# The first group's upper output columns as one seven-product block, with the second group's lower columns inside it

## The chip, the cores and the metric

The kernel runs on one core of a Trainium2 chip. The metric is the device time of one execution in microseconds (us): the median of three runs before is 1700.65 (1699.88 to 1701.31). Engines are named as in the profile: PE (matrix multiply) and PEld (its weight loads), DVE (vector engine), ACT (scalar engine), POOL (GpSimd), SP (sync engine); each works through its own queue in order. SP's queue issues nearly all loads, POOL's the few that add to what lies in memory.

## The reference

One decoder layer for 256 tokens (S) of width 2048 (D), in float32: a SwiGLU FFN of half weight, a mixer, a second such FFN, with RMS norms between. What matters here is the mixer's end:

```
y = concatenate([rms_norm(y_lru, lru_out_norm[l]),
                 rms_norm(y_sc, sc_out_norm[l])], axis=-1)
x = x + y @ w_out[l]
x = x + FFN_RESIDUAL_SCALE * swiglu_ffn(rms_norm(x, ffn2_norm[l]), ...)
```

`y` has two groups of 1024 columns, each with a norm of its own, so the 2048 rows of `w_out` fall into two halves of the K dimension: rows 0 to 1023 belong to the first group, 1024 to 2047 to the second. Each half's product is scaled by its group's norm factor (one number per token) and added to the residual `x`.

## The kernel before

**Units.** A weight matrix is read in units of 512 rows by 512 columns (1 MiB), each by one DMA from SP (line 165) into one of three `raw` buffers. For full precision a unit is split in two: ACT casts it to the matmul's format (`hi`, two casts of half a unit), DVE subtracts (`lo = raw - hi`); there are two `hi`/`lo` buffer pairs (in the FFNs a third, used in every third turn). The activations are split likewise and lie transposed, in units of 512 rows: `yT_0`, `yT_1` for the first group and `yT_2`, `yT_3` for the second, each with both token tiles (t = 0, 1, of 128 tokens). `multiply` runs, for each token tile, 8 matmuls with `hi` and later 4 with `lo`, each 128x128 by 128x512: 24 matmuls for a unit and both tiles, 12 for one tile. Nearly all instructions carry line 43, that of a helper, so they are told apart by tiles.

**The output projection** is a loop over column blocks c (512 columns) and groups g in a fixed order: (0,0), (1,0), (0,1), (2,0), (1,1), (3,0), (2,1), (3,1). Each step (`product`) multiplies two units, `o{c}_{g}_{u}`, into two banks of PSUM (`ps_o`), and DVE adds both to the residual `xres` with the group's factor (`r_y0`, `r_y1`; from the tiny products `pst_0` and `pst_1` of the sums of squares `acc`). The first step of group 1 has its first load held until the mixer's last DMA transpose is issued. When a column block has both groups, it is complete, and the second FFN's input is prepared (`n2`): ACT copies the block's residual into `pair`, SP transposes it by DMA, ACT copies it back and scales it into `xT_n2`, DVE makes its `lo`, ACT sums squares (`junk`).

**Seven products.** In the FFNs, blocks of 2 x 2 units by 2 token tiles are done with seven instead of eight unit products (`seven`). With w11, w12 (upper row, first and second column block), w21, w22 (lower row) the weights multiplied are, in the order of the products p0, p4, p5, p6, p2, p3, p1: w11; w11+w12; that +w22; w12+w22; w22; that of p5 +w21; w21. DVE adds the sums into w11 in halves (`joined`), followed by ACT's cast and DVE's subtract of each half; w12+w22, and with `fourth` also the last +w21, are made by a DMA from POOL that adds in memory (`gather`). The activations' sums are made and split once (`seven_of`, `xs`). w11 and w12 lie in two buffers of their own (`kept`). The products go to three or four PSUM banks, a, c, d (and e), and `snap` copies a bank in between (s5, u2, u3) on ACT. With `beside`, four ordinary units of another product stand inside the block (first FFN's and second FFN's down projection, `down_pair`); then bank e isn't used.

**Order.** The program is written in one order, and a scheduler with costs of its own sets the order of the instructions within each engine's queue.

Of the kernel before, what the change touches and what calls it, by code (L numbers as in the profile page):

```python
# [49 lines left out]
def hybrid_block(ctx: ExitStack, tc: tile.TileContext, a: dict, out: bass.AP):  # L50
# [344 lines left out]
    def quad(tile):  # L395
        return tile.rearrange("p (j c) -> p j c", j=UK)

    def seven(w, rows, cols, sf, xs, name, keep, done, between=None, ready=None, whole=True, order=False, fourth=False, beside=None):
# [562 lines left out]
    with tc.tile_pool(name="mixer", bufs=1) as mp, tc.tile_pool(name="mixw", bufs=2) as mw:  # L961
# [15 lines left out]
        zx, gv, hs, vs, ds, ts, cc, ys, xcs = ({} for _ in range(9))  # L977
# [211 lines left out]
        n2 = Norm("n2", vec["ffn2_norm"])  # L1189
        w_out, turn = a["w_out"][0], held["turn"]  # L1190
        rs = []
        for c, g in [(0, 0), (1, 0), (0, 1), (2, 0), (1, 1), (3, 0), (2, 1), (3, 1)]:
            cs = slice(c * CW, (c + 1) * CW)
            if c == 0 and g == 1:
                flush()
            ps = product(w_out, c, (2 * g, 2 * g + 1), yT.__getitem__, f"o{c}_{g}", turn if (c, g) == (0, 1) else None)
# [9 lines left out]
            for t in range(NT):
                xr = xres[:, t, cs]
                dve.scalar_tensor_tensor(xr, ps[t], rs[g][:, t : t + 1], xr, op0=ALU.mult, op1=ALU.add)
            if g == 1:
                n2.later(c, lambda name: tmp("T", name, 4 * S)[:, :CW], False)  # L1210
# [91 lines left out]
```

## Time and profile before

| | |
|---|---|
| median of the runs | 1700.65 us |
| the profiled execution's own time | 1699.97 us |
| its span, first to last instruction | 1698.2 us |
| granted PE clock | 0.999 |
| busy: PE, DVE, ACT | 99%, 85%, 72% |
| output projection on PE | 919.87 to 1007.92 us of the span |
| input projection before it, second FFN behind it | up to 919.87, from 1007.92 |

Rows of a timeline give the start, the duration, the engine, the operation with output and input tiles, the count, and in brackets the idle time before and what ended it. Names lose their buffer numbers there: `ps_o`, `hi_o` and `raw_o` are the projection's, `hi_d_p` is the `hi` of one of seven products of a down projection.

### The profile page before, as it was taken

The numbers are of one execution on the slowest core, as the hardware profiler recorded it, in microseconds if no ns is written. First come the engines' busy times: TensorE is split into PE (matmuls) and PEld (weight loads), VectorE is DVE, ScalarE is ACT, GpSimd is POOL, SyncE is SP. The second block draws the span as 40 slices with busy tenths as digits, with TensorE's granted clock in tenths as the row PEclk, the third lists the DMA queues.
The fourth block names the chain that finished last, engine by engine and source line by source line (L and its number), as shares of the span: only waits on it lengthen the run. The fifth ranks groups of instructions, "written<-read, shape, count | busy, mean of one in ns | idle before, by whom it ended". The sixth has DMA issues, their size and how long they took to land.

```text
span 1698.2 us, 19673 instructions
## 1 busy us (share of the span) xinstructions
PE 1682.9 (99%) x7447; PEld 1391.6 (82%) x7447; DVE 1442.5 (85%) x1295; ACT 1228.1 (72%) x1534; POOL 47.9 (3%) x52
## 2 busy tenths in 40 slices
PE   8999999999999999999999999999999999999998
PEld 7888888888887888888888888888888888888886
DVE  7998988988988888768696669979889889899787
ACT  7867667758668677977877687776668578678764
POOL 1000000000000000000000000000000000000000
PEclk9999999999999999999999999999999999999999
DMA  8778679788788886875667587787778988888873
GB/s 304 239 249 228 221 245 244 234 256 241 232 279 230 253 262 160 249 215 195 206 203 223 196 248 220 240 249 223 247 234 236 271 234 239 249 246 247 247 226 124
DMA packets 271070, 396.67 MB, mean 234 GB/s; under 512 B 86404, under 2 KB 88832, under 8 KB 270848
## 3 DMA queue, kind: packets, MB, share of 16 engines
q1 hardware_dynamic: 253472, 360.49, 66.1%
q0 software_dynamic: 17216, 33.63, 11.5%
q8 instruction: 58, 0.95, 0.2%
q10 hardware_dynamic: 288, 1.31, 0.2%
q14 instruction: 36, 0.29, 0.1%
HBM read 373.37 MB, written 2.10 MB: 221 GB/s over the span
## 4 chain that ended last, share of the span: by engine, by line
PE 97%; DVE 2%; issue 0%; DMA 0%; ACT 0%; DVEq 0%; SPq 0%; ACTq 0%
PE ps_d L43 14%; PE ps_in L43 13%; PE ps_u_a L43 10%; PE ps_g_a L43 9%; PE ps_u_c L43 6%; PE ps_d_a L43 6%; PE ps_g_c L43 6%; PE ps_o L43 5%; PE ps_g_d L43 5%; PE ps_u_d L43 5%; PE ps_d_c L43 4%; PE ps_u_e L43 3%; PE ps_g_e L43 3%; PE ps_g L43 3%; PE ps_u L43 2%; PE ps_d_d L43 2%
## 5 line engine op out<-in xcount | busy, mean ns | idle before, releaser
L43 ACT CAST hi_u_p<-raw_u 128x1024 fp32r<-128x1024 f32 x140 | 143.0, 1046 | 79.6 <-PE ps_u_a L43 27.8
L43 DVE TENSOR_TENSOR lo_g_p<-raw_g,hi_g_p 128x2048 fp32r<-128x2048 f32 (+1 forms) x84 | 153.1, 1831 | 31.8 <-ACT hi_g_p L43 30.9
L43 DVE TENSOR_TENSOR lo_u_p<-raw_u,hi_u_p 128x2048 fp32r<-128x2048 f32 (+1 forms) x90 | 161.6, 1813 | 21.4 <-ACT hi_u_p L43 20.5
L43 PE MATMUL ps_d<-hi_d,h 128*128 128x512 f32 x704 | 167.2, 389 | 0.0
L43 ACT CAST hi_d_p<-raw_d 128x1024 fp32r<-128x1024 f32 x112 | 115.0, 1047 | 68.0 <-DVE raw_d L43 21.0
L43 ACT CAST hi_g_p<-raw_g 128x1024 fp32r<-128x1024 f32 x132 | 134.8, 1046 | 40.4 <-DVE raw_g L43 24.1
L43 PEld LDWEIGHTS ps_d<-hi_d,h 128*128 128x128 f32 x704 | 132.1, 188 | 27.4
L43 PE MATMUL ps_in<-hi_in,xT_nm 128*128 128x512 f32 x640 | 152.0, 390 | 0.0
L43 PEld LDWEIGHTS ps_in<-hi_in,xT_nm 128*128 128x128 f32 x640 | 119.5, 188 | 24.5
L43 DVE TENSOR_TENSOR lo_d_p<-raw_d,hi_d_p 128x2048 fp32r<-128x2048 f32 (+1 forms) x72 | 129.3, 1812 | 9.3 <-ACT hi_d_p L43 7.7
L43 DVE TENSOR_TENSOR lo_in<-raw_in,hi_in 128x2048 fp32r<-128x2048 f32 x40 | 91.2, 2286 | 45.3 <-ACT hi_in L43 44.9
L43 DVE TENSOR_TENSOR lo_d<-raw_d,hi_d 128x2048 fp32r<-128x2048 f32 x44 | 100.4, 2287 | 22.6 <-ACT hi_d L43 22.5
L43 ACT CAST hi_d<-raw_d 128x1024 fp32r<-128x1024 f32 x88 | 89.2, 1045 | 28.2 <-DMA raw_d<-in_ffn_w_down_dram 10.9
L43 ACT CAST hi_u_x<-raw_u 128x1024 fp32r<-128x1024 f32 x80 | 81.2, 1047 | 35.6 <-PE ps_u_c L43 26.2
L43 ACT CAST hi_in<-raw_in 128x1024 fp32r<-128x1024 f32 x80 | 80.7, 1047 | 27.5 <-PE ps_in L43 22.5
L43 ACT CAST hi_g_x<-raw_g 128x1024 fp32r<-128x1024 f32 x80 | 81.4, 1045 | 17.8 <-DMA raw_g<-in_ffn_w_gate_dram 8.6
L43 DVE TENSOR_TENSOR lo_g_x<-raw_g,hi_g_x 128x2048 fp32r<-128x2048 f32 x40 | 91.4, 2285 | 2.8 <-ACT hi_g_x L43 2.8
L43 DVE TENSOR_TENSOR lo_u_x<-raw_u,hi_u_x 128x2048 fp32r<-128x2048 f32 x40 | 91.4, 2285 | 1.4 <-ACT hi_u_x L43 1.3
L43 PE MATMUL ps_d<-lo_d,h 128*128 128x512 f32 x352 | 87.3, 389 | 0.0
L43 PE MATMUL ps_in<-lo_in,xT_nm 128*128 128x512 f32 x320 | 79.0, 389 | 0.0
L43 PEld LDWEIGHTS ps_d<-lo_d,h 128*128 128x128 f32 x352 | 66.1, 188 | 13.7
L43 DVE TENSOR_TENSOR raw_u<-raw_u,raw_u 128x1024 f32<-128x1024 f32 (+1 forms) x50 | 70.5, 1434 | 5.2 <-DMA raw_u<-in_ffn_w_up_dram 4.9
(405 smaller groups left out, 3683.3 us busy)
## 6 DMA issues: line engine op xcount, KB each, us to landing
raw_d<-in_ffn_w_down_dram SPq DMA_DIRECT2D x88, 1024.0 KB, 5.7
raw_u<-in_ffn_w_up_dram SPq DMA_DIRECT2D x87, 1024.0 KB, 5.2
raw_g<-in_ffn_w_gate_dram SPq DMA_DIRECT2D x86, 1024.0 KB, 5.5
raw_in<-in_w_in_dram SPq DMA_DIRECT2D x40, 1024.0 KB, 5.1
raw_o<-in_w_out_dram SPq DMA_DIRECT2D x16, 1024.0 KB, 5.5
raw_d<-in_ffn_w_down_dram POOLq DMA_DIRECT2D x12, 1024.0 KB, 8.3
raw_g<-in_ffn_w_gate_dram POOLq DMA_DIRECT2D x10, 1024.0 KB, 8.6
raw_u<-in_ffn_w_up_dram POOLq DMA_DIRECT2D x10, 1024.0 KB, 8.3
```

The costliest lines, as they stand in the source:

```text
L43: ins = getattr(self.engine, name)(*args, **kwargs)
```

## The change

Columns 1024 to 2047 (c = 2, 3) of the first group become one seven-product block named `ob`: rows (0, 1) of units, column blocks 2 and 3. The four units of the second group for c = 0 and 1 stand inside it (`Beside`). The order of the projection is now (0,0), (1,0), block with (0,1) and (1,1) inside, (2,1), (3,1). The block's sums of activations are made by `first_group_sums` from `yT_0` and `yT_1`, in the buffers of the mixer's v and d. Its third `hi`/`lo` pair and w11 (`kept_o`) take three of the ten `big` buffers, and w12 (`T_kept`) takes the mixer's T, whose two halves are now one tile; the crossings of `n2` move from T's buffers to the `tok` ones. w11's load is held until the last mixer transpose is issued, as the first load of group 1 was before; w12's is not held and waits for the last reader of T.

```diff
-    def product(w, c, us, y, name, after=None):
+    def product(w, c, us, y, name):
...
-            with tc.issue_after(after.ins) if after and i == 0 else ExitStack():
-                blk = unit(w[u * UK * P : (u + 1) * UK * P, cs], f"{name}_{u}")
+            blk = unit(w[u * UK * P : (u + 1) * UK * P, cs], f"{name}_{u}")
...
-        w11, first = ready or (get(r0, 0, True), None)
+        with tc.issue_after(first_load.ins) if first_load else ExitStack():
+            w11, first = ready or (get(r0, 0, True), None)
...
-                ts[half] = tmp("T", half, 4 * S)
+                both["T"] = both.get("T") or tmp("T", "both", 8 * S, bufs=1)
+                ts[half] = both["T"][:, half * 4 * S : (half + 1) * 4 * S]
...
-        for c, g in [(0, 0), (1, 0), (0, 1), (2, 0), (1, 1), (3, 0), (2, 1), (3, 1)]:
...
-            ps = product(w_out, c, (2 * g, 2 * g + 1), yT.__getitem__, f"o{c}_{g}", turn if (c, g) == (0, 1) else None)
...
+        def onto(c, g, t, *parts):
+            xr = xres[:, t, c * CW : (c + 1) * CW]
+            for p in parts:
+                dve.scalar_tensor_tensor(xr, p, rs[g][:, t : t + 1], xr, op0=ALU.mult, op1=ALU.add)
+
+        def column_done(c):
+            n2.later(c, lambda name: tmp("tok", name, CW, bufs=3), False)
+
+        def whole_product(c, g):
+            ps = product(w_out, c, (2 * g, 2 * g + 1), yT.__getitem__, f"o{c}_{g}")
+            if len(rs) == g:
+                group_factor(g)
+            for t in range(NT):
+                onto(c, g, t, ps[t])
+            if g == 1:
+                column_done(c)
+
+        def first_group_sums():
+            rows = [tmp(tag, "yv", 4 * S, bufs=1) for tag in "vd"]
+            for i in range(2):
+                y = f32(yT[i])
                 for t in range(NT):
+                    dve.tensor_tensor(
+                        quad(rows[t][:, i * CW : (i + 1) * CW]),
+                        y[:, :, t * P : (t + 1) * P], y[:, :, S + t * P : S + (t + 1) * P], op=ALU.add,
+                    )
+            so, two = {}, [big(f"xs_o_{i}") for i in range(2)]
+            rest = seven_of(
+                so, yT[0], yT[1],
...
+        def first_group_block(so, rest):
...
+                def load(i):
+                    c, u = i // 2, 2 + i % 2
+                    return load(w_out[u * UK * P : (u + 1) * UK * P, c * CW : (c + 1) * CW], f"o{c}_{u}")
...
+                def multiply(i, raw):
+                    c, u = i // 2, 2 + i % 2
+                    if u == 2:
+                        side[c] = [bank(f"ps_o{c}_{t}") for t in range(NT)]
+                    blk = parts_of(raw, f"o{c}_{u}")
+                    multiply([(side[c][t], stationary(yT[u], t), u == 2, u == 3) for t in range(NT)], blk, True)
+                    pump(1.5)
+                    if u == 3:
+                        if len(rs) == 1:
+                            group_factor(1)
+                        for t in range(NT):
+                            onto(c, 1, t, side[c][t])
+                        column_done(c)
...
+            def add(t, n, ps, tiles):
+                onto(2 + n, 0, t, *([] if ps is None else [ps]), *tiles)
...
+            extra.extend((
+                Given(hi=big("hi_o"), lo=big("lo_o")),
+                Given(kept=[f32(big("kept_o")), tmp("T", "kept", 8 * S, bufs=1).rearrange("p (j c) -> p j c", j=UK)]),
+            ))
+            seven(
+                w_out, (0, 1), (2 * CW, 3 * CW), so, [], "ob", keep, add, within, fourth=True, beside=Beside, first_load=turn,
+            )
+            extra.clear()
...
+        whole_product(0, 0)
+        sums_of_first = first_group_sums()
+        whole_product(1, 0)
+        flush()
+        first_group_block(*sums_of_first)
+        for c in (2, 3):
+            whole_product(c, 1)
```

What the scheduler made of it, at three places. On PE, from the last product before the block (columns 512 to 1023 of group 0) on, before:

```order
L43 MATMUL ps_o1_0_1_7061<-lo_o1_0_1_7101,yT_1_5359 128x512 x4
L43 MATMUL ps_o0_1_0_7131<-hi_o0_1_2_7135,yT_2_5360 128x512 x8
L43 MATMUL ps_o0_1_1_7132<-hi_o0_1_2_7135,yT_2_5360 128x512 x8
L43 MATMUL ps_o0_1_0_7131<-lo_o0_1_2_7136,yT_2_5360 128x512 x4
L43 MATMUL ps_o0_1_1_7132<-lo_o0_1_2_7136,yT_2_5360 128x512 x4
```

and now (`ps_ob_a`, `ps_ob_c` are the block's banks, `hi_ob_p0` the `hi` of product p0, `hi_o` the third buffer pair, here for the inner unit `o0_2`):

```order
L43 MATMUL ps_o1_0_1_7072<-lo_o1_0_1_7112,yT_1_5359 128x512 x4
L43 MATMUL ps_ob_a_7146<-hi_ob_p0_7163,yT_0_5358 128x512 x8
L43 MATMUL ps_ob_a_7146<-lo_ob_p0_7164,yT_0_5358 128x512 x4
L43 MATMUL ps_ob_c_7147<-hi_ob_p4_7181,xs_o_0_7065 128x512 x4
L43 MATMUL ps_o0_0_7213<-hi_o_7142,yT_2_5360 128x512 x3
L43 MATMUL ps_ob_c_7147<-hi_ob_p4_7181,xs_o_0_7065 128x512 x4
L43 MATMUL ps_ob_c_7147<-lo_ob_p4_7182,xs_o_0_7065 128x512 x2
```

p0 and p4 of the block stand where the first group-1 unit stood, and the inner unit `o0_2` is mixed into p4; behind them come `pst_1` and p5, mixed with the inner unit `o0_3`.

On DVE, from the first group's norm factor on, before:

```order
L43 SCALAR_TENSOR_TENSOR xres_76<-ps_o0_0_1_6953,r_y0_7051,xres_76 128x512
L43 TENSOR_TENSOR lo_o1_0_1_7101<-raw_o1_0_1_7098,hi_o1_0_1_7100 128x2048
L43 TENSOR_TENSOR lo_o0_1_2_7136<-raw_o0_1_2_7133,hi_o0_1_2_7135 128x2048
L43 SCALAR_TENSOR_TENSOR xres_76<-ps_o1_0_0_7060,r_y0_7051,xres_76 128x512
L43 SCALAR_TENSOR_TENSOR xres_76<-ps_o1_0_1_7061,r_y0_7051,xres_76 128x512
L43 TENSOR_TENSOR lo_o0_1_3_7167<-raw_o0_1_3_7164,hi_o0_1_3_7166 128x2048
```

and now (`kept_o` is w11, `T_kept` w12, `raw_ob_11` w22):

```order
L43 SCALAR_TENSOR_TENSOR xres_76<-ps_o0_0_1_6952,r_y0_7050,xres_76 128x512
L43 TENSOR_TENSOR lo_o1_0_1_7112<-raw_o1_0_1_7109,hi_o1_0_1_7111 128x2048
L43 TENSOR_TENSOR lo_ob_p0_7164<-kept_o_7144,hi_ob_p0_7163 128x2048
L43 TENSOR_TENSOR xs_o_0_7065<-v_yv_7059,xs_o_0_7065 128x4x128
L43 SCALAR_TENSOR_TENSOR xres_76<-ps_o1_0_0_7071,r_y0_7050,xres_76 128x512
L43 SCALAR_TENSOR_TENSOR xres_76<-ps_o1_0_1_7072,r_y0_7050,xres_76 128x512
L43 TENSOR_TENSOR kept_o_7144<-kept_o_7144,T_kept_7145 128x1024 x2
L43 TENSOR_TENSOR xs_o_1_7066<-d_yv_7060,xs_o_1_7066 128x4x128
L43 TENSOR_TENSOR lo_ob_p4_7182<-kept_o_7144,hi_ob_p4_7181 128x1024 x2
```

The two half-adds for p4 come behind both residual updates of columns 512 to 1023, and the second of them is what the first adding DMA on POOL (w22 into `T_kept`) waits for.

On ACT, behind the casts of the last unit before the block, before:

```order
L43 CAST hi_o0_1_2_7135<-raw_o0_1_2_7133 128x1024 x2
L43 CAST hi_o0_1_3_7166<-raw_o0_1_3_7164 128x1024 x2
L43 CAST hi_o2_0_0_7219<-raw_o2_0_0_7217 128x1024 x2
L43 CAST hi_o2_0_1_7256<-raw_o2_0_1_7254 128x1024 x2
L43 ACTIVATE s_y1_7201<-v_y1_7200 128x2
```

and now:

```order
L43 CAST hi_ob_p0_7163<-kept_o_7144 128x1024 x2
L43 CAST xs_o_1_7066<-v_yv_7059 128x4x128
L43 CAST hi_o_7142<-raw_o0_2_7151 128x1024 x2
L43 CAST hi_ob_p4_7181<-kept_o_7144 128x1024
L43 COPY ps_ob_d_7148<-ps_ob_a_7146 128x512
L43 CAST hi_ob_p4_7181<-kept_o_7144 128x1024
L43 ACTIVATE ctok_s5_ob_7202<-ps_ob_c_7147 128x512
L43 CAST hi_o_7142<-T_kept_7145 128x1024 x2
L43 CAST hi_ob_p5_7242<-kept_o_7144 128x1024 x2
L43 CAST hi_o0_3_7265<-raw_o0_3_7155 128x1024 x2
```

The casts of p6 (`hi_o` from `T_kept`, which the adding DMA writes and which the inner unit `o0_2` has to release) stand ahead of those of p5.

More of the change, by code (lines that the diff above doesn't have):

```diff
@@ L396, in quad, with seven @@
         return tile.rearrange("p (j c) -> p j c", j=UK)
-    def seven(w, rows, cols, sf, xs, name, keep, done, between=None, ready=None, whole=True, order=False, fourth=False, beside=None):
+    def seven(w, rows, cols, sf, xs, name, keep, done, between=None, ready=None, whole=True, order=False, fourth=False, beside=None, first_load=None):
         a, c, e, d = (bank(f"ps_{name}_{n}") if n != "e" or not beside else None for n in "aced")
@@ L976, in hybrid_block @@
         cw, scw = vec["lru_conv_w"], vec["sc_conv_w"]
-        zx, gv, hs, vs, ds, ts, cc, ys, xcs = ({} for _ in range(9))
+        zx, gv, hs, vs, ds, ts, cc, ys, xcs, both = ({} for _ in range(10))
         def tmp(tag, name, w=S, dt=F32, bufs=2):
@@ L1191, in hybrid_block, with group_factor @@
         rs = []
-        for c, g in [(0, 0), (1, 0), (0, 1), (2, 0), (1, 1), (3, 0), (2, 1), (3, 1)]:
-            cs = slice(c * CW, (c + 1) * CW)
-            if c == 0 and g == 1:
-                flush()
-            ps = product(w_out, c, (2 * g, 2 * g + 1), yT.__getitem__, f"o{c}_{g}", turn if (c, g) == (0, 1) else None)
-            if c == 0:
-                pst = bank(f"pst_{g}")
+        def group_factor(g):
+            pst = bank(f"pst_{g}")
+            for t in range(NT):
+                pe.matmul(pst[:, t : t + 1], acc[:, g, t * P : (t + 1) * P], ones[:, :1], start=True, stop=True)
+            tot = work.tile([P, NT], F32, tag="tot", name=f"tot_y{g}")
+            dve.tensor_copy(tot, pst[:, :NT])
+            rs.append(inv_sqrt(tot, D // 2, f"y{g}"))
@@ L1199, in hybrid_block @@
+        def first_group_sums():
+            rows = [tmp(tag, "yv", 4 * S, bufs=1) for tag in "vd"]
+            for i in range(2):
+                y = f32(yT[i])
                 for t in range(NT):
-                    pe.matmul(
-                        pst[:, t : t + 1], acc[:, g, t * P : (t + 1) * P], ones[:, :1], start=True, stop=True
-                    )
-                tot = work.tile([P, NT], F32, tag="tot", name=f"tot_y{g}")
-                dve.tensor_copy(tot, pst[:, :NT])
-                rs.append(inv_sqrt(tot, D // 2, f"y{g}"))
@@ L1206, in hybrid_block @@
[L1206 to L1210, printed above, removed]
+                    dve.tensor_tensor(
+                        quad(rows[t][:, i * CW : (i + 1) * CW]),
+                        y[:, :, t * P : (t + 1) * P], y[:, :, S + t * P : S + (t + 1) * P], op=ALU.add,
+                    )
@@ new lines, in first_group_sums, with __init__, tile @@
+            so, two = {}, [big(f"xs_o_{i}") for i in range(2)]
+            rest = seven_of(
+                so, yT[0], yT[1],
+                lambda t, i: quad(rows[t][:, i * CW : (i + 1) * CW]),
+                quad(tmp("tok", "yspare", CW, bufs=3)),
+                [(b[:, :, o : o + P], b[:, :, o + P : o + S]) for b in two for o in (0, S)],
+            )
+            return so, rest
+        class Given:
+            def __init__(self, **tiles):
+                self.tiles = tiles
+            def tile(self, shape, dt, tag, name, bufs):
+                return self.tiles[tag].pop(0) if tag == "kept" else self.tiles[tag]
@@ new lines, in first_group_block, with keep, within @@
+        def first_group_block(so, rest):
+            side = {}
+            class Beside:
+                @staticmethod
+                def load(i):
+                    c, u = i // 2, 2 + i % 2
+                    return load(w_out[u * UK * P : (u + 1) * UK * P, c * CW : (c + 1) * CW], f"o{c}_{u}")
+                @staticmethod
+                def multiply(i, raw):
[8 more added lines that the diff above has]
+                            group_factor(1)
+                        for t in range(NT):
+                            onto(c, 1, t, side[c][t])
+                        column_done(c)
+            def keep(name):
+                if name.startswith("u3"):
+                    return tmp("g", name, UK * S, bufs=1)[:, :CW]
+                return tmp("ctok", name, CW)
+            def add(t, n, ps, tiles):
+                onto(2 + n, 0, t, *([] if ps is None else [ps]), *tiles)
+            def within(i):
+                if i == 0:
+                    rest()
+            count = turn_of["split"]
+            turn_of["split"] = 0
+            extra.extend((
[6 more added lines that the diff above has]
+            extra.clear()
+            turn_of["split"] = count
```

## The prediction

> **What bounds the kernel now.** First the page: busy time by engine, and the shares of the chain of waits.
>
> ```profile
> PE 1682.9 (99%) x7447; PEld 1391.6 (82%) x7447; DVE 1442.5 (85%) x1295; ACT 1228.1 (72%) x1534; POOL 47.9 (3%) x52
> PE 97%; DVE 2%; issue 0%; DMA 0%; ACT 0%; DVEq 0%; SPq 0%; ACTq 0%
> ```
>
> TensorE is the chain for 97% of the span. Then the windows of the stretches that the change touches (start of the output projection, the rest of it, the first 42 us of the second FFN) and the PE timeline in it.
>
> ```profile
> core 0: us, PE busy (x) PEld busy (x) DVE busy (x) ACT busy (x) POOL busy (x), PEclk, DMA share, GB/s
> 919.80:942.00 22.20, 22.20 (x102) 18.40 (x101) 16.44 (x26) 17.74 (x25) 0.00 (x0) 1.00 0.63 194
> 942.00:1008.00 66.00, 66.00 (x295) 54.70 (x294) 41.77 (x52) 46.67 (x73) 0.00 (x0) 1.00 0.73 225
> 1008.00:1050.00 42.00, 42.00 (x189) 34.86 (x188) 40.31 (x57) 31.49 (x45) 0.00 (x0) 1.00 0.76 262
> ```
>
> ```profile
> 936.70 3.79 PE L43 MATMUL ps_o<-hi_o,yT 128*128 128x512 f32 x16
> 940.32 1.98 PE L43 MATMUL ps_o<-lo_o,yT 128*128 128x512 f32 x8
> 942.14 3.79 PE L43 MATMUL ps_o<-hi_o,yT 128*128 128x512 f32 x16
> 1007.92 3.79 PE L43 MATMUL ps_g<-hi_g,xT_n 128*128 128x512 f32 x16
> ```
>
> PE has no gap: 24 matmuls (one weight unit for both token tiles) take 942.14 - 936.70 = 5.44 us, 0.227 us each. DVE is about 65% busy and ACT 71% in the projection; behind it DVE is full, 40.31 of 42 us. So a matmul less is worth 0.227 us, and whatever makes PE wait costs its whole length.
>
> **The change part by part.** *Removed:* seven products instead of eight, 12 of the 384 projection matmuls: 12 x 0.227 = **-2.7 us**. That is the most the projection itself can give.
>
> *Start of the block.* p0's matmuls follow the last one of columns 512 to 1023, so PE is ready for p0 at 942.14 and for p4 at 944.86. Rows for what p4 needs:
>
> ```profile
> 928.04 0.37 SPq L165 DMA_DIRECT2D raw_o<-in_w_out_dram  x1
> DMA to landing us min/median/max: 7.6/7.6/7.6
> 935.45 1.41 DVE L43 SCALAR_TENSOR_TENSOR xres<-ps_o,r_y,xres 128x512 f32<-128x512 f32 x2
> 936.78 4.48 DVE L43 TENSOR_TENSOR lo_o<-raw_o,hi_o 128x2048 fp32r<-128x2048 f32 x2
> 317.22 0.68 DVE L43 TENSOR_TENSOR hs<-z,hs 128x512 fp32r<-128x512 f32 x1
> 320.62 2.35 DVE L43 TENSOR_TENSOR raw_d<-raw_d,raw_d 128x1024 f32<-128x1024 f32 x2
> ```
>
> The first row is the load after the last mixer transposes; the new load of kept_o is issued right behind one like it, at about 928.5. The landing is that of the FFN load issued 0.5 us behind another (1007.05), so kept_o lands at about 936.1. ACT then has to finish the last unit's casts and two 0.5 us ones for the sums: p0's casts run about 937.1 to 939.0. DVE is the late one. An extra 0.7 us subtract for a sum (the hs row) moves the two xres updates to about 936.1; then lo of the last unit (2.24, from the x2 row) to 939.7, lo of p0 to 941.9, a subtract to 942.6, two xres updates to 943.9 and the first of the two half-adds, 1.15 each, to 945.05. ACT's cast of that half takes 1.05 (the 327.67 row below): p4 starts at 946.2, 1.3 late. Neighbours on an engine overlap by some hundredths in the rows, and the chain has a dozen of them, so I take **+1.1 us**. Bounds: 0 if DVE's chain is 1.3 shorter, 2.5 if the load lands at 938, 2 us later (DVE's order behind it is fixed).
>
> *The accumulating DMA in front of p5.* The second add lets POOL start the DMA that adds w22 into T_kept (for p6). ACT's order has p6's casts from T_kept ahead of p5's, in one queue, so p5 waits for that DMA. The like place in the first FFN's down block:
>
> ```profile
> 322.96 1.98 PE L43 MATMUL ps_d_a<-hi_d_p,h 128*128 128x512 f32 x8
> 323.63 1.29 POOL L410 DMA_DIRECT2D raw_d<-in_ffn_w_down_dram  x1 [39.55 <-DVE u_g L43]
> 327.67 1.05 ACT L43 CAST hi_d_p<-raw_d 128x1024 fp32r<-128x1024 f32 x1 [0.23 <-DVE raw_d L43]
> 332.27 2.00 ACT L43 CAST hi_d_p<-raw_d 128x1024 fp32r<-128x1024 f32 x2 [0.22 <-PE ps_d L43]
> DMA to landing us min/median/max: 8.1/8.3/11.0
> ```
>
> The adds ended there at 322.97 and POOL began 0.66 later; twelve such DMAs took 8.1 to 11.0 us. p5's casts (from 327.67) stand ahead of p6's (332.27), so nothing waits. Here: with the second add over at A (about 946.2, which is also where p4 starts), the DMA lands at A + 0.7 + 8.3 = A + 9.0, p6's two casts end at A + 10.95, p5's first half at A + 11.9. PE is ready for p5 after p4 and the inner unit, 36 x 0.227 = 8.2, and 0.35 for pst: A + 8.5. **+3.4 us** (3.2 at 8.1; 6.1 at 11.0), and 0.1 for the next unit's first cast. If the DMA did not matter, the casts would still wait for the inner unit to release hi_o, which happens 28 matmuls, 6.35 us, and 0.2 after A: p5 at A + 9.5, +1.0. That is the lower bound.
>
> [...] The twelve accumulating ones above took at least 8.1, so the row goes into the sum.
>
> *After the block.* Columns 0 to 1023 are now complete only inside it, so ACT's work on them (copies for the transposes, squares, scaling) moves late. Its rates and the places that it feeds:
>
> ```profile
> 997.33 1.04 ACT L43 COPY pair<-xres 128x1024 uint16<-128x1024 uint16 x1
> 998.28 0.63 ACT L43 ACTIVATE junk_n<-xres 128x512 f32<-128x512 f32 x1
> 1001.82 1.34 ACT L43 COPY pair<-T_cross_n 128x1024 uint16<-128x1024 uint16 x1
> 1003.04 1.03 ACT L43 CAST hi_g<-raw_g 128x1024 fp32r<-128x1024 f32 x1
> 1003.98 1.27 ACT L43 ACTIVATE xT_n<-pair,cols_many 128x128 fp32r<-128x128 f32 x4
> 1005.16 1.35 ACT L43 COPY pair<-T_cross_n 128x1024 uint16<-128x1024 uint16 x1
> 1009.74 2.29 DVE L43 TENSOR_TENSOR lo_u<-raw_u,hi_u 128x2048 fp32r<-128x2048 f32 x1
> 1013.36 3.79 PE L43 MATMUL ps_u<-hi_u,xT_n 128*128 128x512 f32 x16
> 1064.60 1.07 PE L43 MATMUL ps_g_a<-lo_g_p,xs 128*128 128x512 f32 x4
> 1066.17 0.50 PE L43 MATMUL ps_g_e<-hi_g_x,x 128*128 128x512 f32 x1 [0.49 <-ACT x L43]
> 1070.29 1.07 PE L43 MATMUL ps_g_e<-lo_g_x,x 128*128 128x512 f32 x4
> ```
>
> From starts: copy out 0.95, squares 0.62 (by the overlap of their neighbours), copy back 1.22, cast 0.95, four scalings 1.18. From the first copy of columns 0 to 511 to the second cast of the second FFN's first up-unit ACT's order holds 7, 8, 6, 15 and 6 of these: 6.7 + 5.0 + 7.3 + 14.3 + 7.1 = 40.4 us, without a pause. It can begin only when the xres updates are through, which DVE runs behind lo of p3, and p3 reads the second accumulating DMA. Counted from p5's start S: lo of p5 ends at S + 3.6, that DMA lands 0.7 + 8.3 later, casts 1.95, lo 2.25, the updates 1.6: S + 18.3; the casts end at S + 58.7. PE reaches that unit 252 matmuls, 57.2 us, after S and its second half 0.9 later, so about +0.5 there, and lo_u ends 3.8 after PE's start instead of 1.3 before it (1012.03 against 1013.36): DVE is 5 us later to PE than before. DVE being full, little is made up: 1.5 in two idle spots and the 0.5 that PE waited leave 3. PE waits for DVE there already: the 20 matmuls from 1064.60 to 1070.29 took 5.69 instead of 4.54. The new order does that place's x units ahead of one 2.2 us lo, so 0.7 of the 3 is left: **+1.2 us** in all, between -1.2 (today's wait gone) and +4.
>
> *Costed at nothing:* the first weight piece (T_kept) is loaded ahead of the last input-projection unit, once the last T reader is done. It is covered by slack at the place where loads already delay a transpose; uncovered it costs what one more load adds, 7.6 - 5.5 = 2.1:
>
> ```profile
> DMA to landing us min/median/max: 5.1/5.5/6.6
> 909.50 1.35 ACT L43 COPY g_b<-tok_b 128x1024 uint16<-128x1024 uint16 x1 [4.31 <-DMA tok_b<-pair]
> 912.38 1.03 ACT L43 CAST hi_in<-raw_in 128x1024 fp32r<-128x1024 f32 x1
> 914.43 3.79 PE L43 MATMUL ps_in<-hi_in,xT_nm 128*128 128x512 f32 x16
> ```
>
> That cast ends at 913.4 and its half is read four matmuls into the group, at 915.3: 1.9 of slack, 0.2 at stake. Sums and their casts before 935 fall into DVE and ACT pauses. Three more conversions and two more loads are within the 29% and 27% that ACT and DMA leave free.
>
> **Sum:** -2.7 + 1.1 + 3.5 + 1.2 = **+3.1**. The profiled execution (span 1698.2, its time 1699.97, 0.7 under the median) would become about 1701.3 and 1703.1; on the median of 1700.65 that is **1703.7 us**, 0.18% slower. A measurement here tells about 0.2% (3.4 us) from no change, so this counts as no difference, just inside.
>
> **Rivals.**
> 1. *The saving arrives.* The other down blocks run gapless with the same seven products, which speaks for it; against it, their p5 casts stand ahead of p6's and their adds ended before p0 began. Time 1700.65 - 2.7 = 1698.0; with today's wait at 1066 gone as well, 1696.8.
> 2. *The first DMA is hidden,* the hi_o release decides: 3.4 becomes 1.0, 1701.3. Against it, the 8.1 minimum.
> 3. *The second accumulating DMA is late.* Place: p3's casts, behind them the saturated ACT chain and the full DVE. The second such DMA of the down blocks took the 11.0 of the row, beside the loads that follow it. From 7.8 us on (8.3 less the 0.5 that PE waits in the forecast) each further us goes to PE: 11.0 - 8.3 = 2.7, 1706.4, slower than before.
> 4. *The clock drops in p5's gap.* After its one long idle, at the start, PE runs at half rate for a while:
>
> ```profile
> 5.77 1.97 PE L43 MATMUL pt_n<-ident,xres 128*128 128x128 f32 x8 [2.92 <-DMA xres<-in_x_dram]
> 8.55 0.63 PE L43 MATMUL ps_g<-lo_g_start,xT_n 128*128 128x512 f32 x1
> 8.97 1.05 PE L43 MATMUL ps_g<-hi_g_start,xT_n 128*128 128x512 f32 x2
> ```
>
>    One matmul takes 0.42 there (8.55 to 8.97), twice 0.227. Nine of them cost 1.8: 1705.5, from an idle of about 2.9 on. Against it: the windows' granted clock is 1.00, and a cold start isn't a gap in dense work. [...]
>
> **How the numbers follow.** Forecast 0.50 (its own range 1701.9 to 1705.6), saving arrives 0.12, first DMA hidden 0.10, second late 0.17, clock 0.11. Faster by over 0.2% (below 1697.25) needs the second form of rival 1: 0.05. Slower by over 0.2% (above 1704.05): rivals 3 and 4, 0.28, and a little over a third of the forecast's own range, 0.18: 0.46. The rest, 0.49, is within. The range leaves out most of rival 1 below and a late DMA together with a late p4 above: 1699.5 to 1707.0.
>
> **What would show it.** In the profile after: twelve matmuls fewer; PE waiting about 1.1 at ps_ob_c for ACT's hi_ob and about 3.4 at ps_ob_a for the p5 casts; ACT idle before hi_o<-T_kept until a DMA; ACT without a pause from the first copy of xres to hi_u; the wait at the first gate block about 1 us longer. If PE is gapless in the block, or p6's casts don't wait for the DMA, the forecast is wrong by the step named; if the time is right but PE waits elsewhere, it was luck.

## The result and the profile after

The changed kernel takes 1712.71 us (median of 6 runs, 1711.31 to 1713.65) against 1700.48 for the kernel before on the same chip: ratio 1.0072, 95% interval 1.0059 to 1.0084. It is 12.2 us slower. 1703.7 was forecast, with a range up to 1707.0: the sign of the likeliest case held, the size did not. All runs told of here were fast ones; a single slow run, of the control before_sq, is left out of its median.

The page of the profile after, busy time:

```profile
span 1711.1 us, 19691 instructions
PE 1685.2 (98%) x7435; PEld 1389.0 (81%) x7435; DVE 1461.5 (85%) x1318; ACT 1238.1 (72%) x1548; POOL 50.5 (3%) x54
```

PE has the 12 matmuls less (7435 against 7447) and yet a span 12.9 us longer; its busy time grew by 2.3 only, so nearly all of the loss is waiting. The windows of the stretches that the prediction showed, after the change:

```profile
core 0: us, PE busy (x) PEld busy (x) DVE busy (x) ACT busy (x) POOL busy (x), PEclk, DMA share, GB/s
919.80:942.00 22.20, 21.92 (x99) 17.85 (x99) 18.91 (x31) 19.57 (x29) 0.00 (x0) 1.00 0.78 250
942.00:1008.00 66.00, 60.53 (x261) 49.42 (x260) 52.08 (x60) 45.61 (x66) 2.60 (x2) 0.97 0.69 195
1008.00:1050.00 42.00, 40.39 (x179) 32.89 (x178) 34.30 (x53) 35.10 (x56) 0.00 (x0) 1.00 0.89 271
```

PE was busy all of the time here before; now it idles 5.5 us in the second row, and the granted clock there is 0.97. The third row now begins 6 us ahead of the second FFN, so it can't be set beside the one before as it stands. Over 42 us from the FFN's first matmul, in both kernels, DVE is busy for 36.74 us instead of 40.31 and ACT for 34.17 instead of 31.49. DVE, which was full there, now has pauses, and all that it waits for from 1008 to 1080 is ACT (8.6 us together).

Two stretches are compared throughout, both between matmul starts: the *projection*, from the first `ps_o` to the second FFN's first `ps_g` (920.54 to 1014.06 now), and the *tail* from there to the end of the span. "Lost" is the time by which matmuls start later than 0.227 us after the one ahead, wherever a step is over 0.25.

| stretch | before | after | forecast |
|---|---|---|---|
| start of the projection | 919.87 | 920.54 | no change |
| projection | 88.05 (0.2 lost) | 93.53 (8.2 lost) | +1.9 |
| tail | 690.26 (1.3 lost) | 697.01 (7.7 lost) | +1.2 |

So +5.5 and +6.7 were measured where +1.9 and +1.2 were forecast. The 0.67 at the start lie in what the edit doesn't touch: the first matmul starts 0.46 later, a wait in the first FFN at 173 us costs 0.63, and other waits are shorter. PE's timeline after the change, the places that lose in the projection:

```profile
941.43 2.11 PE L43 MATMUL ps_o<-lo_o,yT 128*128 128x512 f32 x8 [0.28 <-DVE lo_o L43]
945.20 1.07 PE L43 MATMUL ps_ob_a<-lo_ob_p,yT 128*128 128x512 f32 x4
947.84 1.20 PE L43 MATMUL ps_ob_c<-hi_ob_p,xs_o 128*128 128x512 f32 x4 [1.57 <-ACT hi_ob_p L43]
956.14 0.50 PE L43 MATMUL pst<-ones,acc 128*128 128x1 f32 x4
960.54 3.47 PE L43 MATMUL ps_ob_a<-hi_ob_p,xs_o 128*128 128x512 f32 x8 [3.90 <-ACT hi_ob_p L43]
963.80 1.58 PE L43 MATMUL ps_o<-hi_o,yT 128*128 128x512 f32 x5
```

PE waits 1.57 us for p4 and 3.90 for p5, as named. Then p5's eight matmuls fill 960.54 to 963.80, 0.41 us each instead of 0.227, and the next ones are slow until 964.2: the clock dropped (rival 4), granted 0.55 from 960.54 to 964.20. What p5 waited for, on POOL's and ACT's timelines:

```profile
948.42 1.29 POOL L409 DMA_DIRECT2D T_kept<-in_w_out_dram  x1 [97.41 <-DVE xs_o L43]
964.79 1.30 POOL L409 DMA_DIRECT2D kept_o<-in_w_out_dram  x1 [15.07 <-PE ps_ob_a L43]
```

```profile
957.55 1.99 ACT L43 CAST hi_o<-T_kept 128x1024 fp32r<-128x1024 f32 x2 [5.14 <-DMA T_kept<-in_w_out_dram]
959.44 1.99 ACT L43 CAST hi_ob_p<-kept_o 128x1024 fp32r<-128x1024 f32 x2
974.52 2.00 ACT L43 CAST hi_o<-kept_o 128x1024 fp32r<-128x1024 f32 x2 [3.59 <-DMA kept_o<-in_w_out_dram]
979.49 1.05 ACT L43 CAST hi_o<-raw_o 128x1024 fp32r<-128x1024 f32 x1 [2.48 <-DMA raw_o<-in_w_out_dram]
980.45 1.04 ACT L43 COPY pair<-xres 128x1024 uint16<-128x1024 uint16 x1
1013.49 2.57 ACT L43 COPY pair<-tok_cross_n 128x1024 uint16<-128x1024 uint16 x2 [1.13 <-DMA tok_cross_n<-pair]
1021.39 1.03 ACT L43 CAST hi_u<-raw_u 128x1024 fp32r<-128x1024 f32 x1
```

The first accumulating DMA takes 9.1 us from POOL's issue to p6's casts; p5's casts start only at 959.44, behind them. The second one holds p3's casts until 974.52, 9.7 us after its issue. ACT's work on the now late columns runs from 980.45 to the second cast of the first up-unit, which ends at 1022.42: 42.0 us (40.4 forecast). PE's waits behind the projection:

```profile
1020.91 1.20 PE L43 MATMUL ps_u<-hi_u,xT_n 128*128 128x512 f32 x4 [1.25 <-ACT hi_u L43]
1022.47 3.01 PE L43 MATMUL ps_u<-hi_u,xT_n 128*128 128x512 f32 x12 [0.36 <-ACT hi_u L43]
1054.18 2.12 PE L43 MATMUL ps_g<-lo_g,xT_n 128*128 128x512 f32 x8 [1.03 <-DVE lo_g L43]
1069.55 2.11 PE L43 MATMUL ps_g_c<-hi_g_x,x 128*128 128x512 f32 x8 [0.56 <-ACT s_g L43]
1074.33 1.20 PE L43 MATMUL ps_g_a<-hi_g_p,xs 128*128 128x512 f32 x4 [0.85 <-ACT hi_g_p L43]
1076.22 1.20 PE L43 MATMUL ps_g_a<-hi_g_p,xs 128*128 128x512 f32 x4 [0.69 <-ACT hi_g_p L43]
```

### The profile page after: what moved, and what is told of

Its sections match the earlier page's. It is cut to its first block, busy times and chain, and to the rows that moved or that the text cites. A ratio compares the mean times of both kernels' runs of the same rounds, so it can differ in the third digit from the quotient of the medians.

```text
span 1711.1 us, 19691 instructions
## 1 busy us (share of the span) xinstructions
PE 1685.2 (98%) x7435; PEld 1389.0 (81%) x7435; DVE 1461.5 (85%) x1318; ACT 1238.1 (72%) x1548; POOL 50.5 (3%) x54
## 5 line engine op out<-in xcount | busy, mean ns | idle before, releaser
L43 DVE TENSOR_TENSOR lo_u_p<-raw_u,hi_u_p 128x2048 fp32r<-128x2048 f32 (+1 forms) x90 | 161.4, 1813 | 17.7 <-ACT hi_u_p L43 17.0
L43 ACT CAST hi_g_p<-raw_g 128x1024 fp32r<-128x1024 f32 x132 | 134.6, 1048 | 38.3 <-DVE raw_g L43 23.8
L43 ACT CAST hi_d<-raw_d 128x1024 fp32r<-128x1024 f32 x88 | 89.1, 1046 | 25.5 <-DMA raw_d<-in_ffn_w_down_dram 10.3
L43 PE MATMUL ps_d<-lo_d,h 128*128 128x512 f32 x352 | 87.3, 389 | 0.0
```

The lines of the kernel that those rows point to most:

```text
L43: ins = getattr(self.engine, name)(*args, **kwargs)
```

## The experiments

Theory from the profile after: three separate losses, (1) p5 behind p6 on ACT, with the slow matmuls behind it, (2) the DVE chain in front of p4, (3) ACT too late and too full behind the block. Rivals: the DMA is late in whatever order; the slow matmuls have a cause of their own; the tail is a matter of loads. All times are medians; projection and tail come from each kernel's profiled execution, one of the runs. The kernels ran in six batches, each with runs of the kernel before beside it (medians 1699.85 to 1700.57), so the ratios compare best.

| kernel | us (runs) | ratio to before, 95% | projection | tail |
|---|---|---|---|---|
| changed | 1712.71 (6) | 1.0072, 1.0059 to 1.0084 | 93.5 | 697.0 |
| p5_first | 1707.10 (4) | 1.0041, 1.0026 to 1.0056 | 88.0 | 697.2 |
| fill_gap | 1709.92 (4) | 1.0054, 1.0039 to 1.0069 | 94.4 | 695.0 |
| late_columns | 1706.01 (7) | 1.0031, 1.0019 to 1.0042 | 88.1 | 697.1 |
| no_squares | 1705.91 (7) | 1.0034, 1.0023 to 1.0045 | 92.9 | 690.9 |
| second_add | 1704.85 (9) | 1.0024, 1.0013 to 1.0034 | 88.4 | 694.2 |
| sq_dve | 1705.24 (10) | 1.0029, 1.0019 to 1.0040 | 88.9 | 694.9 |
| all3 | 1703.87 (10) | 1.0017, 1.0008 to 1.0026 | 86.9 | 693.8 |
| all4 | 1700.26 (10) | 0.9995, 0.9985 to 1.0004 | 88.3 | 689.8 |
| all5 | 1698.78 (11) | 0.9991, 0.9982 to 1.0000 | 87.3 | 690.4 |
| all6 | 1702.26 (12) | 1.0012, 1.0003 to 1.0020 | 86.7 | 692.2 |
| all8 | 1704.52 (7) | 1.0031, 1.0019 to 1.0042 | 86.8 | 695.7 |
| before_sq | 1701.95 (10) | 1.0006, 0.9997 to 1.0015 | 88.1 | 692.0 |

### p5's casts ahead of p6's

```diff
-        product_of(6, w12, a)
+        with tc.issue_after(cast5.ins) if beside else ExitStack():
+            product_of(6, w12, a)
```

`cast5` is the second cast of p5.

> p6's two casts are held behind p5's second cast on ACT; nothing else is edited. Theory (queue): in the changed kernel p5 waits only because p6's casts stand ahead of it and wait for the accumulating DMA. With p5's casts first they can start when the second add ends, about the time PE ends the inner unit, so the idle of 3.9 us in front of ps_ob_a shrinks to under 1 us, and with it go the nine matmuls at 0.43 us behind it: 3.9 + 1.9 less, projection 93.5 to about 88, time about 1707 us. Rival (the DMA is late whatever the order): p6 then waits for it in place of p5, PE idles 2 us or more in front of p6, and the time is 1710 or more. Rival (the wait only moves behind the projection, since ACT's work there starts from the second DMA): the projection gains 5 and the stretch from the second FFN's first matmul on loses as much, time 1711 to 1713.

PE's timeline at p4 and p5, and ACT's at p3 and the first copy:

```profile
946.17 1.19 PE L43 MATMUL ps_ob_c<-hi_ob_p,xs_o 128*128 128x512 f32 x4 [0.93 <-ACT hi_ob_p L43]
954.46 1.07 PE L43 MATMUL ps_ob_a<-hi_ob_p,xs_o 128*128 128x512 f32 x4
955.37 1.07 PE L43 MATMUL ps_o<-hi_o,yT 128*128 128x512 f32 x4
```

```profile
967.68 2.00 ACT L43 CAST hi_o<-kept_o 128x1024 fp32r<-128x1024 f32 x2 [4.61 <-DMA kept_o<-in_w_out_dram]
976.17 1.05 ACT L43 COPY pair<-xres 128x1024 uint16<-128x1024 uint16 x1 [1.34 <-DVE xres L43]
```

p5 starts with no wait, and no matmul behind it is slow; the projection falls by 5.5 us and the time by 5.6. Not all of the 5.5 is the order's: the wait for p5 and the slow matmuls had cost 5.8, of which 1.4 come back as two waits for ACT's casts at 991.0 and 992.5, and 1.2 were gained ahead of p5, at p4 and the `lo` before it. The theory (queue) holds: the DMA itself was in time for p6, and only the order made p5 wait for it. The tail keeps all of its loss, so it does not come from p5's wait. The p4 stall is 0.93 here. In the changed kernel the last mixer transposes landed later, and the chain of p4 with them; ACT's copies behind these transposes, there and in this kernel:

```profile
927.98 2.56 ACT L43 COPY g_b<-tok_b 128x1024 uint16<-128x1024 uint16 x2 [1.62 <-DMA tok_b<-pair]
```

```profile
926.27 2.60 ACT L43 COPY g_b<-tok_b 128x1024 uint16<-128x1024 uint16 x2 [0.36 <-DMA tok_b<-pair]
```

In the six kernels that keep DVE's order there (changed, p5_first, fill_gap, no_squares, second_add, sq_dve) p4 starts 19.9 us after the first of these copies, whether the copy is early or late. Why the transposes land later in some executions isn't shown: SP's order of issue is the same in the two shown.

### Work in the gap

```diff
+        if first_load:
+            beside.fill()
         blk, _ = joined(5, w22,
...
+                    with tc.issue_after(held["last"].ins):
+                        for _ in range(18):
+                            pe.matmul(idle, yT[0][:, 0, :P], yT[1][:, 0, :], start=True, stop=True)
```

> 18 extra matmuls (fp32r, 128x512, into a bank that nobody reads) stand on PE between the inner unit o0_2 and p5, about 4.1 us of work in the 3.9 us that PE idles there; ACT's order of p6 before p5 is kept. Theory (the idle itself lowers the rate): with PE busy through the gap, p5's matmuls start at 0.227 us each, the nine at 0.43 us are gone, and the kernel is 1.5 to 2 us faster than the changed one in spite of 18 more matmuls: about 1711. Rival (the slow matmuls have another cause, for example the operands that have just been written, or the DMA traffic): the matmuls behind the gap stay at 0.43 us and the time is 1712.5 to 1713.5.

```profile
956.04 4.24 PE L43 MATMUL idle<-yT,yT 128*128 128x512 f32 x18
960.36 2.14 PE L43 MATMUL ps_ob_a<-hi_ob_p,xs_o 128*128 128x512 f32 x8
962.86 0.74 PE L43 MATMUL ps_ob_a<-lo_ob_p,xs_o 128*128 128x512 f32 x2 [0.37 <-DVE lo_ob_p L43]
964.00 0.73 PE L43 MATMUL ps_ob_a<-lo_ob_p,xs_o 128*128 128x512 f32 x2 [0.40 <-DVE lo_ob_p L43]
```

The idle is filled and the eight matmuls of p5 run at full rate, about 0.24 us each: 960.36 to about 962.3 instead of 3.3 us. So the slow matmuls followed from the idle. But they cost little on the path: at full rate PE reaches p5's `lo` before DVE has made it and loses 1.3 us there (four late starts), of the 1.8 that the slow rate cost. From p5's start to the end of the projection this kernel takes 53.7 us, the changed one 53.5 and p5_first 53.6. The 2.8 us by which the median fell do not come from the clock: between the profiled executions the projection is 0.8 longer, the tail 2.0 shorter (the scheduler put instructions behind the block in another order) and the start 0.9 earlier. So the rate is explained as expected, but the time that was expected for it came from elsewhere.

### Late columns without the block

```diff
-        for c, g in [(0, 0), (1, 0), (0, 1), (2, 0), (1, 1), (3, 0), (2, 1), (3, 1)]:
+        for c, g in [(0, 0), (1, 0), (2, 0), (0, 1), (3, 0), (1, 1), (2, 1), (3, 1)]:
```

This is the kernel before; the hold for the last transpose and the flush move to the third step with it.

> The kernel before with its eight ordinary products in another order: 0, 1 and 2 of the first group, 0 of the second, 3 of the first, 1, 2, 3 of the second. No seven-product block, no accumulating DMA, no sums. Columns 0 to 511 and 512 to 1023 are complete 192 and 96 matmuls before the end of the projection (240 and 144 before, 192 and 108 in the changed kernel). Theory (late columns saturate ACT): the stretch from the second FFN's first matmul to the end grows by 5 to 7 us as in the changed kernel (697.0 against 690.3), the projection stays at 88: time 1705 to 1708. Rival (the block itself is late, by its loads and its DMAs, and delays what follows): the tail grows by no more than 1.5 us, time 1700.5 to 1702.

```profile
1045.63 3.78 PE L43 MATMUL ps_u<-lo_u,xT_n 128*128 128x512 f32 x8 [4.26 <-DVE lo_u L43]
```

```profile
1037.27 0.68 DVE L43 TENSOR_TENSOR spare<-v,v 128x512 f32<-128x512 f32 x1
1042.09 1.28 DVE L43 TENSOR_TENSOR x<-v,x 128x512 fp32r<-128x512 f32 x2
1043.30 2.28 DVE L43 TENSOR_TENSOR lo_u<-raw_u,hi_u 128x2048 fp32r<-128x2048 f32 x1
```

The tail grows by 6.9 us with no block at all, so columns that are complete later, with the order that the scheduler then makes, can cost that much. But it is not the mechanism that was to be tested: the loss sits in one place, where DVE's queue has the pieces of the gate block's operands (`v`, `x`, `xs`) ahead of a `lo_u`, and the matmuls behind this 4.26 us idle are slow, too (3.78 us for eight instead of 1.98). As a test of ACT's saturation it is inconclusive.

### ACT relieved, work left out

```diff
+            if self.name == "n2":
+                return
             for t, engine in enumerate(engines):
...
         n2 = Norm("n2", vec["ffn2_norm"])
+        dve.memset(n2.ss, float(CW))
```

> The changed kernel without the eight squares (with their sums) of the second FFN's norm, which is given a constant in their place: 8 x 0.62 = 5.0 us less work on ACT between the first copy of xres and the second FFN's first up-unit; the output changes by the norm's factor. Theory (ACT's unbroken work sets the tail): hi_u is ready 3 to 5 us earlier, PE's 1.25 and 0.36 us in front of ps_u go, and most of the waits for DVE at 1052 to 1076 us: the tail shrinks by 3 to 5 us, time 1707.5 to 1709.5. Rival (late loads or DMA traffic set the tail): the time stays within 1 us of the changed kernel's 1712.7.

```profile
1018.99 3.79 PE L43 MATMUL ps_u<-hi_u,xT_n 128*128 128x512 f32 x16
```

With 5.0 us less on ACT the tail is 690.9, all but 0.6 of its loss undone, more than the 3 to 5 expected. No load was touched, so the rival of late loads falls. That relief of 5 us brings back 6.1 fits the chain: DVE waits for ACT up to the first up-unit and is full behind it, so it carries ACT's lateness into the waits at 1054 to 1076. The fourth `lo_u` of the second FFN, just ahead of the gate block, shows it, in the kernel before and in the changed one:

```profile
1041.85 2.28 DVE L43 TENSOR_TENSOR lo_u<-raw_u,hi_u 128x2048 fp32r<-128x2048 f32 x1
```

```profile
1054.05 2.29 DVE L43 TENSOR_TENSOR lo_u<-raw_u,hi_u 128x2048 fp32r<-128x2048 f32 x1
```

Counted from the FFN's first matmul that is 33.9 and 40.0 us, 6.1 later; the first `lo_u` was 6.6 later, so DVE made up only 0.5 between the two. Without the squares it is 34.3. In all 14 kernels the tail goes with this start: it is 690.9 or less where the start is 34.3 or less, 692.0 to 695.7 at 35.6 to 37.2, and 695.0 to 697.2 at 38.3 to 40.3.

The edit doesn't single out ACT's work, though. Without squares the norm's factor doesn't wait for the last columns either (`r_n` is made 17.7 us before the FFN's first matmul instead of 11.2 after it), and the scheduler put DVE's work in another order, the third `lo_u` ahead of the gate block's pieces.

### The second sum on DVE, and the squares on DVE

Both contain p5_first. The first drops `fourth=True` (DVE adds w21, no second accumulating DMA):

```diff
-                w_out, (0, 1), ..., keep, add, within, fourth=True, beside=Beside, first_load=turn,
+                w_out, (0, 1), ..., keep, add, within, beside=Beside, first_load=turn,
```

> p5's casts first, as in p5_first, and p3's operand is summed by one more DVE add (kept_o plus w21, 128x2048, about 2.3 us) in place of the second accumulating DMA; one megabyte less is moved. Theory (the second DMA holds back column 0): in p5_first ACT idles 4.6 us for that DMA in front of p3's casts, a copy that DVE waits for stands behind them, and so xres of columns 0 to 511 is updated at 975.4 to 976.7 though PE ended those products at 962.6. Without the DMA the first copy of xres starts 4 us or more earlier (976.2 becomes 972 or less), ACT's unbroken work ends as much earlier, and the tail shrinks from 697.2 by 3 to 5 us: time 1702 to 1704. Rival (ACT's amount of work sets the tail, whenever it starts; DVE's extra add costs its length): tail 696.5 to 699, time 1706.5 to 1709.

```profile
968.25 0.60 ACT L43 ACTIVATE g_u_ob<-ps_ob_a 128x512 f32<-128x512 f32 x1 [2.99 <-PE ps_ob_a L43]
971.31 1.05 ACT L43 CAST hi_o<-raw_o 128x1024 fp32r<-128x1024 f32 x1 [2.37 <-DMA raw_o<-in_w_out_dram]
975.11 1.04 ACT L43 COPY pair<-xres 128x1024 uint16<-128x1024 uint16 x1
```

The tail falls by 3.0 us, as expected at the lower end, and the waits for `ps_u` are gone; the time falls by 2.3, less than expected, and the step to it was smaller: the first copy starts at 975.11, counted from the start of the projection (920.50, 920.09 in p5_first) 1.5 us earlier and not 4. ACT's last wait is now the load for the last inner unit (2.37), but DVE's update of `xres`, which the copy needs, ended only at 974.8, so the load held it for 0.3.

The second moves the squares:

```diff
+                if self.name == "n2":
...
+                    dve.scalar_tensor_tensor(junk, x, 1.0, x, op0=ALU.mult, op1=ALU.mult, accum_out=part)
```

> p5's casts first, as in p5_first, and the eight squares of the second FFN's norm on DVE instead of ACT: 5.0 us less on ACT, about 8 x 0.75 = 6.0 us more on DVE; nothing is left out. Theory (ACT is the late engine up to the second FFN's first up-unit, where DVE waited 9 us for it; DVE is full behind it): PE's 2.0 and 0.5 us in front of ps_u shrink to under 0.5, and the waits at the gate block behind (1046 to 1071 us, 3.7 us together) shrink by half or more, since DVE starts into it earlier: tail 692 to 694.5, time 1702 to 1704.5. Rival (DVE is the bound of the whole stretch, and ACT's lateness is only what DVE shows): 6 us more on DVE leave the tail at 697 or make it longer, time 1707 to 1711.

```profile
1063.74 3.64 PE L43 MATMUL ps_g_c<-hi_g_x,x 128*128 128x512 f32 x8 [2.57 <-ACT s_g L43]
```

PE no longer waits for `ps_u`, but at the gate block behind it waits 2.57 us at once and then runs eight matmuls at 0.43 us each. Tail and time come out just above what the theory gave and below the rival: ACT was late at the up-unit, DVE is the bound behind it, and both count. The runs of this kernel scatter from 1701.59 to 1711.25; tail and waits are those of one at 1705.90.

### All of it together

all3 is second_add with the two updates of columns 512 to 1023 written behind p4's adds; all4 adds the squares on DVE; all5 moves the updates of columns 0 to 511 likewise.

```diff
             def within(i):
                 if i == 0:
                     rest()
+                    for put in late:
+                        put()
```

> second_add, and the two xres updates of columns 512 to 1023 of the first group are written behind the adds for p4 instead of ahead of them. Theory (DVE's chain in front of p4): the 1.4 us of the two updates leave the chain, PE's stall in front of ps_ob_c (1.1 in p5_first, 1.7 in the changed kernel) falls below 0.3, and the projection takes about 86.5 (85.3 would be no stall); together with what second_add brings, time 1700.5 to 1703. Rival (the load of kept_o is what p4 waits for): the stall stays, and the time is that of second_add within 0.5 us.

> all3 with the squares on DVE: p5's casts first, the second sum on DVE, the updates behind the adds, the squares moved. If the saving of the block (12 x 0.227 = 2.7 us) is real and only waits hid it, this is the kernel in which it should show: projection about 86, tail 690.3 to 692, time 1697.5 to 1700.5. Rival (the late columns cost the tail something that no relief of ACT undoes, such as the late start of the norm's factor): tail 693 or more, time 1701 or more.

> all4 with the xres updates of columns 0 to 511 of the first group, too, written behind the adds for p4; in the order of DVE's queue that moves one of the two (0.7 us) from in front of lo of the last ordinary unit to behind the adds. Theory (DVE's chain in front of p4 is what is left of the block's stalls): the waits of all4 for that lo (0.64 at 941.5) and for p4 (0.43 and 0.30) shrink by 0.7 together, nothing else moves, time 1699 to 1700.3. Rival (every such edit reshuffles the order behind it, and that moves more than the edit): the tail leaves 689.5 to 690.5, and the time lies outside 1699 to 1700.5.

all3's PE at p4, and all5's at p4, p5 and the first up-unit:

```profile
945.80 2.25 PE L43 MATMUL ps_ob_c<-hi_ob_p,xs_o 128*128 128x512 f32 x8 [0.34 <-ACT hi_ob_p L43]
```

```profile
944.20 2.20 PE L43 MATMUL ps_ob_c<-hi_ob_p,xs_o 128*128 128x512 f32 x8
953.49 1.18 PE L43 MATMUL ps_ob_a<-hi_ob_p,xs_o 128*128 128x512 f32 x4
976.23 2.14 PE L43 MATMUL ps_ob_a<-hi_o,yT 128*128 128x512 f32 x8 [0.93 <-ACT hi_o L43]
1011.98 3.79 PE L43 MATMUL ps_u<-hi_u,xT_n 128*128 128x512 f32 x16
```

p4's stall falls to 0.34 with the updates out of the way although kept_o's load took 9.7 us there. Counted from the first group's factor (`r_y0` on DVE), p4 starts 10.3 us later in the six kernels with the old order, with loads of 7.8 us (p5_first) to 9.7 (changed), and 9.0 in all3, all4 and all5, with loads of 9.7, 9.4 and 7.5: DVE's chain was what p4 waited for, and not the load. all3's time of 1703.87 is 0.9 above what was expected. all4 is level with the kernel before, its tail even 0.5 shorter, with 2.9 still lost in a projection of 88.3 where 86 was expected. all5 is the fastest at 1698.78, 1.4 under the kernel before by the medians, ratio 0.9991 with an interval that ends at 1.0000: a gain at the edge of what these runs can tell. By the traces no more than 0.6 of it is the block's: the projection is 0.7 shorter than in the kernel before, the tail 0.2 longer, and the rest lies ahead of the projection. The waits for that `lo` and in front of p4 are gone, 0.4 stay inside p4 (its four `lo` matmuls take 1.49 us); of the 1.9 us between the spans of all4 and all5, however, 1.6 lie ahead of the projection, where the edit can't be, 0.9 in the projection, and the tail gives 0.6 back. What all5 still loses in the projection is mostly 1.2 in front of p3.

### Controls and two attempts that failed

before_sq is the kernel before with the squares on DVE; all6 is all4 with the first group's norm factor ahead of the first product; all8 is all3 with only the squares of columns 0 to 1023 on DVE.

> The kernel before with one edit: the eight squares of the second FFN's norm on DVE instead of ACT (no block). It tells whether all4 draws level by the block's saving or by the moved squares. Theory (DVE is full behind the projection in the kernel before, 40.3 of 42 us, and ACT is not late there): the squares' 6 us on DVE make the waits at the gate block (0.9 us at 1065) longer, tail 690.3 to 693, time 1700.5 to 1703.5. Rival (the moved squares help the kernel before as much as the changed one, by 4 us): it can give at most the 1.2 us of waits that the tail holds, time 1699.3 to 1700; then all4's block has gained nothing.

> all4 with the factor of the first group's norm (the two pst matmuls, the square root on ACT, the four small DVE instructions) written ahead of the first product instead of behind it. Theory (that chain is what the DVE work in front of p4 still starts from: DVE waits 1.3 us for the square root at 937, behind a 1.3 us table load on ACT): the chain is done before 931, lo of the last unit and the adds for p4 start 1 to 1.5 us earlier, the stalls of all4 at 938 to 950 (2.3 us together) shrink to under 1, projection 86 to 87, time 1698.5 to 1699.8. Rival (the load of the table and the square root then fall between the casts and copies of the last mixer columns, and delay the unit behind them): new stalls at 925 to 937 of 1 us or more, time 1700.5 or more.

> all3 with the squares of columns 0 to 1023 alone on DVE, those of columns 1024 to 2047 left on ACT: half of the relief of all4, at the time at which DVE waits for ACT and not where DVE becomes full (the kernel before lost 1.5 us by all eight on DVE). Theory (ACT must be relieved early, DVE must not be loaded late): tail 688.5 to 690.5, projection 86.5 to 88 as in all3 and all4, time 1698 to 1700.5. Rival (ACT needs the whole relief: the later squares stand in front of the casts for the first up-unit): PE waits 1 us or more for ps_u or at the gate block again, tail 691.5 to 693, time 1701 to 1703.

Moving the squares makes the kernel before 1.5 us slower by the medians (the interval reaches down to 0.9997), its tail 1.8 longer, as expected: all4 doesn't draw level by that edit alone. all6 shortened the projection as expected (86.7) and gave it back in the tail (692.2: 1.5 in front of `ps_g_c` and one wait for the norm's factor); its runs scatter from 1699.53 to 1708.32. In all8 the tail is worse than in all3, against both theories:

```profile
1042.17 3.08 PE L43 MATMUL ps_u<-lo_u,xT_n 128*128 128x512 f32 x8 [2.78 <-DVE lo_u L43]
```

It is the place of late_columns again, a `lo_u` behind the operand pieces in DVE's queue, with slow matmuls behind it (3.08 us for these eight). How the scheduler orders those pieces was not varied by itself, so how much of the tail's 6.7 us in the changed kernel belongs to that order stays open. What is shown is that the loss goes when ACT is relieved and starts earlier (all4, all5, with the factor still made from the squares) and that it is DVE's lateness at the gate block that PE pays for.

## Why the prediction was wrong

Two steps failed: what is left for PE after the block, put at +1.2 and measured at +6.7, and the argument that kept the slow clock out of the sum, 1.8. Two more terms were right in mechanism and too small. In the projection the measured terms add up: -2.7 + 2.4 + 4.0 + 1.8 = +5.5.

- **The saving, -2.7.** Right: 12 matmuls fewer. In all5 the projection is 0.7 shorter than before with 1.9 more lost to waits, which comes to about the 2.7; as time it hardly shows in any kernel.
- **p4, +1.1.** The mechanism (DVE's chain, not the load) is right, by all3 and by the distances from the factor. In p5_first the stall is 1.2 with the step behind it; the changed kernel's execution lost 1.84 there and 0.55 at the `lo` ahead of it, since the mixer's last transposes landed about a microsecond later. Whether the loads that the prediction costed at nothing have a share in that isn't shown: ACT waited over 1.1 us for these transposes in seven of the eleven kernels with the block, in none of the three without it. Inside the bounds of 0 to 2.5 taken together (2.4), undersized by 1.3.
- **The accumulating DMA, +3.5.** Right in mechanism and nearly in size: 4.0 with the step behind it, because the DMA took 9.1 us from POOL's issue to the casts instead of 8.3. p5_first shows it by undoing it.
- **The clock, a rival with 0.11.** It did happen, with the 1.8 us that the rival priced, and the forecast of 3.4 us of idle already lay above the 2.9 from which it was priced there, the idle of 2.92 at the start of the kernel before. The step that failed is the argument against it, that a gap in dense work is not a cold start: after 3.90 us of idle the matmuls took 0.427 us each, and in sq_dve 2.57 us were enough. The 1.8 should have been in the forecast's own sum. fill_gap adds that 1.3 of the 1.8 would have been lost to p5's `lo` at full rate, too: a wait that the sum had not got either.
- **After the block, +1.2.** This is the largest miss: +6.7. The direction was right (ACT without a pause, from late columns), the two steps behind it were not. First, ACT's chain was started at p5 + 18.3 and run "without a pause": it began at p5 + 19.9 and held waits of 0.39 and 1.13 for transposes, so its end lay 3.2 us after the forecast; PE, itself 1.8 later by the slow matmuls, lost 2.2 at `ps_u` instead of 0.5. Of the 1.6 by which it began late, 1.4 is the second accumulating DMA, 9.7 us instead of 8.3: rival 3, in part. The last inner unit's load, which ACT waited 2.48 for and the sum had not got, held the first copy by only 0.2 (DVE's update ended at 980.24). Second, "0.7 of the 3 is left" at the gate block: that place cost 4.4 us instead of the 1.1 of before, 3.3 more and not 0.7. DVE came there 6.1 us late, of which PE had waited 2.2 before; the new order of x units, which was to hide 2.2 of the rest, saved nothing that shows. Of the remaining 1.3, 1.0 is lost further on in the FFN, where the kernels lie between 0.1 and 1.8. all4 and no_squares bring nearly all of the tail back.
- **The chances.** The sum's pieces were added as if each wait ended on its own. Two of them, p5's idle and ACT's lateness, fed others (slow matmuls, DVE's lateness). The terms' own upper ends with the clock, -2.7 + 2.5 + 6.2 + 4 + 1.8 = +11.8, would have reached 1712.5; the range stopped at 1707.0 since it took one late case at a time.

## What to carry to other kernels

When a change delays the point at which a finished block feeds the next stage, count the next stage's work on each engine from that point on, waits included, and if an engine is full behind it, carry its lateness forward at full length instead of letting it fade. Put casts that wait for a slow transfer behind those that are ready: one held pair in an in-order queue cost 5.8 us at its place here, the slow matmuls included, twice the saving that the block could bring. An idle of PE of some 2.6 us or more, by what these kernels show, is best priced with the slow matmuls that follow it.

## What the runs showed of the hardware

PE fell to 0.427 us per matmul after idles in dense work of 2.57 (sq_dve), 2.78 (all8), 3.90 (the changed kernel) and 4.26 us (late_columns), for 7 to 12 matmuls; in all8 the slow steps began only 1.2 us behind the idle. After 1.88 us it did not fall:

```profile
1015.56 1.19 PE L43 MATMUL ps_u<-hi_u,xT_n 128*128 128x512 f32 x4 [1.88 <-ACT hi_u L43]
1017.12 3.02 PE L43 MATMUL ps_u<-hi_u,xT_n 128*128 128x512 f32 x12 [0.37 <-ACT hi_u L43]
```

These rows are p5_first's. Filling the gap of the changed kernel with 18 matmuls avoided the fall: p5's eight took about 0.24 us each in fill_gap.
